# Second products of two feed-forwards as 7 quarter products in place of 8

## The chip, the cores and the metric

One Trainium2 chip, one core. The metric is the device time of one execution in microseconds (us), lower is better. Engines are written as in the profile: PE (TensorE, the products), DVE (VectorE), ACT (ScalarE), POOL (GpSimd), SP (SyncE, which issues most loads).

## The reference, cut to what matters

Two transformer blocks over 256 tokens of width 2048, everything in float32. Each ends in a feed-forward. Of the first block:

```python
z = rmsnorm(h, norm2_w) @ mlp_w1                 # (256, 2048) @ (2048, 8192)
h = h + jnp.square(jax.nn.relu(z)) @ mlp_w2      # (256, 8192) @ (8192, 2048)
```

and of the second, with 5632 hidden features and layer norms around it:

```python
g, u = jnp.split(x @ w_in, 2, axis=-1)           # (256, 2048) @ (2048, 11264)
return (jax.nn.silu(g) * u) @ w_out              # (256, 5632) @ (5632, 2048)
```

In front of these stand the mixers (gated linear attention and pooling in the first block; two kinds of attention, then attention over a memory, in the second).

## The kernel before, in words

Every product of a weight with an activation is done in three float32r products, high x high, high x low and low x high, because a float32 number is kept as a high and a low float32r part that add up to it. `Stream` (L34) loads the weights, tile by tile in the order of use, through SP's queue; a tile holds 128 partitions x 1024 numbers (512 KB). Three raw tiles are loaded ahead (`RAW`), and tiles are split up to three ahead of the product that uses them (`LOOK`, four buffers of each part): ACT copies the high part (L63), DVE subtracts it from the raw tile for the low part (L64).

The kernel first builds a list of jobs (`prog`) and then runs it. A `TJob` has the weights stationary and gives [feature, token]; it is used for a feed-forward's first product. Its tile is 2 blocks of 128 input features x 512 output features, and for each block and 128 features it issues a product of 512 columns and one of 256 (L253 to L257). An `NJob` has the activations stationary and gives [token, feature]; it is used for the second product. Its tile is 2 blocks of hidden features x 512 output features, and for both token tiles and both blocks it issues three products of 512 columns (L273 to L275), 12 a tile. Products accumulate in one of six PSUM banks (`acc`); two more banks (`aux`) belong to side work.

The hidden features of the first feed-forward are done in 8 chunks of 8 blocks of 128, those of the second in five chunks of 8 blocks and one of 4. The order is: first product of chunk c+1 (`up`, `ffn_up`), then second product of chunk c (`down`, `ffn_down`), whose rows are added to the residual `res` chunk by chunk. Four column groups of 512 make up the output's 2048 columns. Between products, `side.pump()` issues pieces of side work: results are read out of a bank in steps (`join` L346 and L360, the square or the gate, `split_steps` L371 and L373). All engines work through their instructions in the order of issue. The final layer norm's rows are loaded from POOL's queue in `last_rows` (a memset of 1.76 us on DVE at L1477).

Of the kernel before, what the change touches and what calls it, by code (L numbers as in the profile page):

```python
# [18 lines left out]
SEQ = 256  # L19
# [10 lines left out]
LOOK = 3  # L30


class Stream:
    """Weight tiles in the order in which the products use them: loaded ahead, and split  # L34
    into two float32r parts (hi + lo == w exactly)."""

    def __init__(self, nc, pool, src, specs, beside):
        self.nc, self.pool, self.src, self.specs, self.beside = nc, pool, src, specs, beside
        self.at = 0
        self.i = self.d = self.s = 0  # L40
        self.raw, self.parts = {}, {}

    def fill(self, ahead=LOOK):
        n = len(self.specs)
        nc = self.nc
        while True:
            moved = False
            if self.d < min(n, self.s + RAW):
                kq, cols, _ = self.specs[self.d]
                t = self.pool.tile([128, kq, cols], F32, name="wraw", tag="wraw", bufs=RAW)  # L50
                nc.sync.dma_start(t, bass.AP(tensor=self.src.tensor, offset=self.src.offset + self.at,
                                             ap=[[kq * cols, 128], [cols, kq], [1, cols]]))
# [5 lines left out]
            if self.s < min(n, self.i + min(ahead, 1 + self.i // 5), self.d):  # L58
                kq, cols, _ = self.specs[self.s]
                t = self.raw.pop(self.s)  # L60
                hi = self.pool.tile([128, kq, cols], F32R, name="whi", tag="whi", bufs=SPLIT)
                lo = self.pool.tile([128, kq, cols], F32R, name="wlo", tag="wlo", bufs=SPLIT)
                nc.scalar.copy(hi, t)  # L63
                nc.vector.tensor_tensor(lo, t, hi.bitcast(F32), op=OP.subtract)  # L64
                self.parts[self.s] = (hi, lo)
                self.s += 1
                moved = True
            if not moved:
                return

    def next(self, fill=True):
        self.i += 1
        if fill or self.i > self.s:
            self.fill()
        return self.parts.pop(self.i - 1)
# [10 lines left out]
class Side:  # L86
    """Work that is issued in small pieces between the products of the main sequence.
    Lanes 0 and 1 have a PSUM bank each; lane 2 is for work that needs none."""
# [11 lines left out]
    def post(self, gen):  # L100
        """A chain of steps on one result; one step at a time, chains in order."""
# [40 lines left out]
def wtile(name, kbs, pieces):  # L142
    """One weight tile: rows of the blocks kbs (consecutive), columns of pieces."""
# [9 lines left out]
def hybrid_two_block_kernel(ctx: ExitStack, tc: tile.TileContext, a, out):  # L153
# [40 lines left out]
    def early(d):  # L194
        """Loads between those of the first weights."""
# [66 lines left out]
    class NJob:  # L262
        """out[token, feature]: activations stationary, weights moving."""
# [13 lines left out]
        def run(self):  # L277
# [23 lines left out]
            # the last steps, of one group: the first token tile as a whole before the second  # L301
# [16 lines left out]
    class Call:  # L318
        """fn at this place of the sequence; what is pending is issued first."""
# [22 lines left out]

    def lo_half(b, scale=None):
# [7 lines left out]
    def join(dst, b, scale=None, rb=None):  # L351
        """dst = scale * (both halves of the bank) * rb, in two steps"""
# [16 lines left out]
    def split_steps(hi, lo, src):  # L369
        yield  # L370
        S.copy(hi, src)  # L371
        yield
        V.tensor_tensor(lo, src, hi.bitcast(F32), op=OP.subtract)  # L373

# [12 lines left out]
    def square_scale(st, eps, name):  # L387
        """Per token 1 / (mean square + eps), along the partitions."""
        def f(lane):
# [8 lines left out]
            rowb[name, "r"] = rs  # L398
        return f
# [23 lines left out]
    def turn_raw(XT, i, g):  # L423
        """Rows of the residual times a weight per feature to XT[feature, block, hi/lo, token]."""
# [16 lines left out]
    class Turn:  # L441
        """LayerNorm of the residual, in place without ln_g and ln_b, and with both to XT."""
# [49 lines left out]
        def spread(self):  # L492
            """As side work."""
# [17 lines left out]
        def begin(self):  # L511
            """At once: the first token tile while the products for the second still run."""
# [20 lines left out]
        def upto(self, n):  # L533
            """At once, as far as block pair n."""
# [8 lines left out]
    # ======================= first block =======================  # L543
# [63 lines left out]
    # pool branch  # L607
# [56 lines left out]
    # gated linear attention  # L664
# [192 lines left out]
    # output projection of the mixer  # L857
# [10 lines left out]
    def add_rows(name, turn=None, rows=None):  # L868
        """Adds to the residual, with its moments; turn: (name, weights) of what reads it next."""
# [33 lines left out]
    # feed-forward of the first block  # L903
# [21 lines left out]
    def relu2(c, at):  # L925
        def f(i, b):
            z = yield from join(None, b)
            V.scalar_tensor_tensor(z, z, 0.0, z, op0=OP.max, op1=OP.mult)
            yield from split_steps(hid[c][:, at + i, 0], hid[c][:, at + i, 1], z)
        return f  # L930

    def up(c):
        Name(set_hid, c, FCH)
        for g in range(FCH // 4):
            t_job("mlp_w1", ALLK, 128 * FCH * c + 512 * g, xt("x2t"), relu2(c, 4 * g),
# [721 lines left out]
```

## Time and profile before

| what | value |
|---|---|
| median of 3 runs | 2546.48 us (2545.93 to 2546.59) |
| span of the profiled execution, first to last instruction | 2543.4 us (its time as a run isn't recorded) |
| PE, PE weight loads, DVE, ACT, POOL busy | 2520.1, 2160.9, 1611.4, 1190.8, 60.6 us |
| weights moved | 460.77 MB of 472.93 MB, through SP's queue |
| mean granted clock of PE | 0.997 |

A busy time is the time in which at least one instruction of the engine was under way. The products overlap each other in their pipeline, so a product's listed duration is longer than the distance between the starts of two. An instruction's idle time ahead of it is named with what ended it. L12 is line 12 of the kernel.

### The profile page before, as it was taken

To read this page: it belongs to the slowest core of one execution; us is meant where nothing else is said; L and a number is where in the kernel's file an instruction comes from. 1 tells how busy PE (TensorE), PEld (TensorE's weight loads), DVE (VectorE), ACT (ScalarE), POOL (GpSimd) and SP (SyncE) were. 2 spreads that over 40 slices of the span, in tenths; PEclk is the share of its full clock that TensorE was granted. 3 is DMA by queue.
4 is the path that set the end of the run, shared out by engine and by line. 5 is a ranking of instruction groups with operands and counts; after the bars stand their busy time and mean duration, and the time that the engine had idled before them with its cause. 6 is when DMAs were issued, how large, how long until landed. Compare 5 with 4: busy or idle time off the path is not lost.

```text
span 2543.4 us, 34921 instructions
## 1 busy us (share of the span) xinstructions
PE 2520.1 (99%) x13581; PEld 2160.9 (85%) x13581; DVE 1611.4 (63%) x2240; ACT 1190.8 (47%) x1680; POOL 60.6 (2%) x82
## 2 busy tenths in 40 slices
PE   8999999999999999999999999999999999999998
PEld 8897888888888888888888888888788888888886
DVE  5655666556656656768656667767775555565557
ACT  5444444444444444444544565555544444444443
POOL 0000000000000000000000000020200000000000
PEclk9999999999999999999999999999999999999999
DMA  8444555555566565555555555665566666566664
GB/s 278 133 160 147 164 190 189 191 191 191 183 198 197 190 193 190 187 168 181 172 174 166 166 185 188 224 218 165 190 190 190 193 189 195 186 197 189 193 193 156
DMA packets 132326, 472.93 MB, mean 186 GB/s; under 512 B 14992, under 2 KB 16352, under 8 KB 131888
## 3 DMA queue, kind: packets, MB, share of 16 engines
q1 hardware_dynamic: 128624, 460.77, 56.5%
q0 software_dynamic: 3104, 9.32, 1.3%
q8 instruction: 106, 1.74, 0.3%
q10 hardware_dynamic: 432, 0.61, 0.1%
q14 instruction: 60, 0.49, 0.1%
HBM read 468.54 MB, written 2.10 MB: 185 GB/s over the span
## 4 chain that ended last, share of the span: by engine, by line
PE 96%; DVE 2%; DMA 1%; ACT 1%; issue 0%; POOL 0%; SPq 0%; DVEq 0%; ACTq 0%; POOLq 0%
PE acc L257 34%; PE acc L256 17%; PE acc L273 11%; PE acc L274 11%; PE acc L275 11%; PE acc L253 2%; PE acc L247 2%; PE acc L249 2%; PE acc L248 2%; DMA wraw<-in_weights_dram 1%; PE acc L254 1%; DVE wlo L64 1%; PE aux L1160 0%; PE aux L1090 0%; ACT whi L63 0%
## 5 line engine op out<-in xcount | busy, mean ns | idle before, releaser
L64 DVE TENSOR_TENSOR wlo<-wraw,whi 128x1024 fp32r<-128x1024 f32 (+1 forms) x870 | 1055.6, 1219 | 856.0 <-ACT whi L63 854.6
L63 ACT CAST whi<-wraw 128x1024 fp32r<-128x1024 f32 (+1 forms) x870 | 905.8, 1047 | 1060.4 <-PE acc L257 507.7
L257 PE MATMUL acc<-x5t,whi 128*128 128x512 f32 x1320 | 462.8, 394 | 1.0 <-DVE x5t L490 1.0
L256 PE MATMUL acc<-x5t,wlo 128*128 128x256 f32 x1320 | 366.7, 278 | 0.0
L257 PE MATMUL acc<-x3t,whi 128*128 128x512 f32 x960 | 339.4, 395 | 0.0
L257 PE MATMUL acc<-x2t,whi 128*128 128x512 f32 x960 | 335.9, 394 | 0.0
L257 PEld LDWEIGHTS acc<-x5t,whi 128*128 128x128 f32 x1320 | 247.8, 188 | 54.7 <-DVE x5t L490 1.4
L256 PE MATMUL acc<-x3t,wlo 128*128 128x256 f32 x960 | 272.0, 283 | 0.0
L256 PE MATMUL acc<-x2t,wlo 128*128 128x256 f32 x960 | 266.1, 277 | 0.0
L256 PEld LDWEIGHTS acc<-x5t,wlo 128*128 128x128 f32 x1320 | 248.1, 188 | 4.3 <-DVE wlo L64 0.2
L257 PEld LDWEIGHTS acc<-x2t,whi 128*128 128x128 f32 x960 | 180.0, 187 | 39.0
L257 PEld LDWEIGHTS acc<-x3t,whi 128*128 128x128 f32 x960 | 180.1, 188 | 38.6
L273 PE MATMUL acc<-whi,hid 128*128 128x512 f32 x512 | 199.5, 390 | 0.0
L274 PE MATMUL acc<-wlo,hid 128*128 128x512 f32 x512 | 199.2, 389 | 0.0
L275 PE MATMUL acc<-whi,hid 128*128 128x512 f32 x512 | 199.2, 389 | 0.0
L256 PEld LDWEIGHTS acc<-x3t,wlo 128*128 128x128 f32 x960 | 181.0, 189 | 3.2
L256 PEld LDWEIGHTS acc<-x2t,wlo 128*128 128x128 f32 x960 | 180.2, 188 | 2.9
L274 PE MATMUL acc<-wlo,fh 128*128 128x512 f32 x352 | 137.1, 389 | 0.5 <-DVE wlo L64 0.5
L273 PE MATMUL acc<-whi,fh 128*128 128x512 f32 x352 | 137.0, 389 | 0.0
L275 PE MATMUL acc<-whi,fh 128*128 128x512 f32 x352 | 136.9, 389 | 0.0
L275 PEld LDWEIGHTS acc<-whi,hid 128*128 128x128 f32 x512 | 96.1, 188 | 20.0
L274 PEld LDWEIGHTS acc<-wlo,hid 128*128 128x128 f32 x512 | 96.1, 188 | 19.9
(481 smaller groups left out, 3577.5 us busy)
## 6 DMA issues: line engine op xcount, KB each, us to landing
wraw<-in_weights_dram SPq DMA_DIRECT2D x859, 512.0 KB, 3.6
row<-in_ln_g_dram POOLq DMA_DIRECT2D x12, 256.0 KB, 6.5
wraw<-in_weights_dram SPq DMA_DIRECT2D x8, 336.0 KB, 2.9
ht<-in_hT_dram SPq DMA_DIRECT2D x8, 272.0 KB, 5.1
res<-in_x_dram SPq DMA_DIRECT2D x2, 1024.0 KB, 8.6
row<-in_ln_b_dram POOLq DMA_DIRECT2D x8, 256.0 KB, 9.3
out_dram<-res SPq DMA_DIRECT2D x6, 256.0 KB, 2.7
pw<-in_pool_w_dram SPq DMA_DIRECT2D x1, 1024.0 KB, 8.7
```

What stands on the lines that cost most here:

```text
L63: nc.scalar.copy(hi, t)
L64: nc.vector.tensor_tensor(lo, t, hi.bitcast(F32), op=OP.subtract)
L247: mm(b[:m, :n], wh, x[:, 0], start=first, stop=False)
L248: mm(b[:m, :n], wh, x[:, 1], start=False, stop=False)
L249: mm(b[:m, :n], wl, x[:, 0], start=False, stop=last)
L253: mm(bv, wh, x, start=True, stop=False, skip_group_check=True)
L254: mm(bv[:, 1], wl, x[:, 0], start=False, stop=False, skip_group_check=True)
L256: mm(bv[:, 1], wl, x[:, 0], start=False, stop=False, skip_group_check=True)
L257: mm(bv, wh, x, start=False, stop=last, skip_group_check=True)
L273: mm(b, xh, hi[:, j, :n], start=first, stop=False)
L274: mm(b, xh, lo[:, j, :n], start=False, stop=False)
L275: mm(b, xl, hi[:, j, :n], start=False, stop=last)
```

## The change

In 15 places, two column groups of a chunk's second product (256 tokens x 1024 hidden features x 1024 output columns) are done as a 2x2 matrix of quarters: four quarters of the activations (128 tokens x 512 hidden features) and four of the weights (512 x 512), with 7 products of quarters (`seven`). Three of these products use sums of weight quarters and four use sums of activation quarters. In the first feed-forward it is column groups 0 and 1 of chunks 0 to 6 (7 places; groups 2 and 3 go on as before in `row_units`), in the second all columns of chunks 0 to 3 (8 places). The last chunks stay as they were.

- The four weight quarters stay in SBUF (`Ring`: five slots of 1 MB, a sixth and later quarter is loaded where an earlier one is done with), are summed in place by DVE, and each product's quarter is split into high and low as the tiles were (`Item`, `Stream.fill`). The sums that a tile needs are issued one tile early, between the high and the low part of the tile in front.
- The sums of activation quarters are made as the hidden features arrive (`four_sums`) and split later (`convert`).
- Products that share a bank leave one product or more between the read of the bank (`put`) and the next product into it. What is common to three output quarters is kept in `u` over all chunks and added once (`add_common`, `add_common_scaled`).
- A first product is done one block of 128 output features at a time (`feature_units`: tiles of 8 input blocks x 128), and its tiles are placed between the steps of `seven` (`merge`).
- The row factor 2^0.25 of the second block's residual goes into the affine step, `last_rows` is issued after the last chunk's first product, and its loads follow each other at a pause of 1 where it was 6.

```diff
 class Stream:
...
+            if self.q < len(self.quads) and self.s > self.quads[self.q].after:
+                q = self.quads[self.q]
+                q.t = q.slot()
+                self.load(q.t, q.at, *q.spec[:2])
+                self.q += 1
                 moved = True
+            if self.s < min(n, self.i + min(ahead, 1 + self.i // 5)):
...
+                    hi = self.pool.tile([128, kq, cols], F32R, name="whi", tag="whi", bufs=SPLIT)
+                    lo = self.pool.tile([128, kq, cols], F32R, name="wlo", tag="wlo", bufs=SPLIT)
+                    nc.scalar.copy(hi, t)
+                    self.pre(self.s + 1)
+                    nc.vector.tensor_tensor(lo, t, hi.bitcast(F32), op=OP.subtract)
+                    if held:
+                        self.sums(it.post)
...
+    def feature_units(W, c0, rhs, evac):
...
+                for j in range(8):
+                    x = rhs(8 * h + j)
+                    wh, wl = hi[:, j], lo[:, j]
...
+                        mm(bv[:, 1], wl, x[:, 0], start=False, stop=False, skip_group_check=True)
+                        mm(bv, wh, x, start=False, stop=h == 1 and j == 7, skip_group_check=True)
...
+    def seven(W, k0, c0, ring, lhs, put):
+        b12, b11, b22, b21 = ring.quads(W, k0, c0)
+        add, sub = OP.add, OP.subtract
+        at = {}
+
+        def unit(name, h, bank, first, then):
+            def run():
+                hi, lo = stream.next()
+                if first and h == 0:
+                    at[bank] = aux(0) if bank == "y" else aux(1) if bank == "x" else acc()
+                b = at[bank]
+                for j in range(2):
+                    xh, xl = lhs(name, 2 * h + j)
+                    mm(b, xh, hi[:, j], start=first and h == 0 and j == 0, stop=False, skip_group_check=True)
+                    mm(b, xh, lo[:, j], start=False, stop=False, skip_group_check=True)
+                    mm(b, xl, hi[:, j], start=False, stop=h == 1 and j == 1, skip_group_check=True)
+                    if h == 1 and j == 1:
+                        put(then, b)
+                    side.pump()
+            return run
+
+        out = []
+        for name, bank, first, then, item in (
+                ("s1", "y", True, "-22", lambda h: Item(b12[h], pre=[(b12[h], b11[h], add)])),
+                ("a11", "x", True, "u", lambda h: Item(b11[h])),
+                ("s2", "u", True, "u+", lambda h: Item(b12[h], pre=[(b12[h], b22[h], add)])),
+                ("a12", "x", False, "+11", lambda h: Item(b21[h], post=[(b21[h], b12[h], add)])),
+                ("s3", "w", True, "-22", lambda h: Item(b12[h], pre=[(b12[h], b11[h], sub)])),
+                ("s4", "y", False, "-12", lambda h: Item(b22[h])),
+                ("a22", "w", False, "+21", lambda h: Item(b21[h]))):
+            for h in range(2):
+                out.append(Unit(item(h), unit(name, h, bank, first, then)))
+        return out
+
+    def merge(head, first, second, tail):
+        n = len(second) - tail
+        done = 0
+        for k, u in enumerate(second):
+            upto = len(first) if k >= n else min(len(first), head + (len(first) - head) * k // max(n - 1, 1))
+            prog.extend(first[done:upto])
...
+    def four_sums(where, i, u, l):
...
+        V.tensor_tensor(sf[:, 0, i], l1, u1, op=OP.subtract)
+        V.scalar_tensor_tensor(sf[:, 1, i], sf[:, 0, i], -1.0, u0, op0=OP.mult, op1=OP.subtract)
+        V.scalar_tensor_tensor(sf[:, 2, i], l0, -1.0, sf[:, 1, i], op0=OP.mult, op1=OP.subtract)
+        V.tensor_tensor(sf[:, 3, i], u0, u1, op=OP.subtract)
...
+    def middle(c):
+        Name(set_hid, c + 1, FCH)
+        ups = up_parts(c + 1)
+        down = seven("mlp_w2", FCH * c, 0, mring, lambda name, j: quarter(sums, hid[c], name, j), put_scaled(c))
+        merge(3 if c == 0 else 2, ups[:SHARE], down, 0)
+        rows = [u for g in (2, 3) for u in row_units("mlp_w2", FCH * c, g, lambda kb: hid[c][:, kb], add_scaled)]
+        merge(1, ups[SHARE:], rows, 2)
...
+    def ffn_middle(c):
+        Name(set_fh, c + 1, chunks[c + 1][1])
+        down = [x for p in range(2) for x in
+                seven("w_ffn_out_2", 8 * c, 1024 * p, ring, lambda name, j: quarter(fh, fh[c], name, j), put_rows(c, p))]
+        merge(5 if c == 0 else 3, up_units(c + 1), down, 4)
...
+    ffn_up()
+    last = len(chunks) - 1
+    Name(lambda: side.finish(tk["affine"]))
+    for c in range(last - 1):
+        ffn_middle(c)
+    Name(set_fh, last, 1)
+    prog.extend(up_units(last))
+    Call(add_common)
+    Name(last_rows)
+    n_job("w_ffn_out_2", range(8 * last - 8, 8 * last), grp, lambda kb: fh[last - 1][:, kb - 8 * last + 8], add_part)
+    n_job("w_ffn_out_2", range(8 * last, 8 * last + 4), grp, lambda kb: fh[last][:, kb - 8 * last], final_rows, tail=2)
```

## Rows read from the trace of the kernel before

**Rows 1.** The page's parts 1 and 2: busy time by engine, PE's clock.

```profile
PE 2520.1 (99%) x13581; PEld 2160.9 (85%) x13581; DVE 1611.4 (63%) x2240; ACT 1190.8 (47%) x1680; POOL 60.6 (2%) x82
...
PEclk9999999999999999999999999999999999999999
```

**Rows 2.** The page's part 4: the chain that ended last, by engine.

```profile
PE 96%; DVE 2%; DMA 1%; ACT 1%; issue 0%; POOL 0%; SPq 0%; DVEq 0%; ACTq 0%; POOLq 0%
```

**Rows 3.** Busy time by stretch: both feed-forwards with several chunks each.

```profile
core 0: us, PE busy (x) PEld busy (x) DVE busy (x) ACT busy (x) POOL busy (x), PEclk, DMA share, GB/s
...
425.00:1043.00 618.00, 618.00 (x3103) 524.36 (x3102) 381.57 (x462) 270.98 (x340) 0.00 (x0) 1.00 0.59 190
...
1978.00:2460.00 482.00, 482.00 (x2545) 413.35 (x2544) 274.06 (x320) 217.32 (x285) 0.00 (x0) 1.00 0.61 191
```

**Rows 4.** Timeline of PE in a second product: first and last of 36 products.

```profile
620.00 0.39 PE L273 MATMUL acc<-whi,hid 128*128 128x512 f32 x1
...
627.93 0.39 PE L275 MATMUL acc<-whi,hid 128*128 128x512 f32 x1
```

**Rows 5.** Timeline of ACT in a first product: first and last of five copies.

```profile
560.90 1.05 ACT L63 CAST whi<-wraw 128x1024 fp32r<-128x1024 f32 x1 [1.73 <-PE acc L257]
...
571.99 1.05 ACT L63 CAST whi<-wraw 128x1024 fp32r<-128x1024 f32 x1 [1.72 <-PE acc L257]
```

**Rows 6.** Timeline of PE and ACT where a second product begins.

```profile
426.24 0.40 PE L257 MATMUL acc<-x2t,whi 128*128 128x512 f32 x1
...
426.47 0.39 PE L273 MATMUL acc<-whi,hid 128*128 128x512 f32 x1
...
434.88 1.05 ACT L63 CAST whi<-wraw 128x1024 fp32r<-128x1024 f32 x1 [0.69 <-PE acc L275]
```

**Rows 7.** Groups of DVE's instructions by form: busy us, mean ns of one.

```profile
L64 DVE TENSOR_TENSOR wlo<-wraw,whi 128x1024 fp32r<-128x1024 f32 x859 | 1047.0, 1224 | 849.6 <-ACT whi L63 848.2
L360 DVE TENSOR_TENSOR ev<-acc,ev 128x256 f32<-128x256 f32 x124 | 51.7, 417 | 0.0
L944 DVE SCALAR_TENSOR_TENSOR res<-acc,rq,res 128x512 f32<-128x512 f32 x56 | 39.3, 743 | 0.0
...
L940 DVE TENSOR_TENSOR res<-acc,res 128x512 f32<-128x512 f32 x32 | 20.6, 682 | 0.0
...
L1114 DVE SCALAR_TENSOR_TENSOR pb<-l1c,pb 128x128 f32<-128x128 f32 x1 | 0.3, 291 | 0.0
...
L1113 DVE TENSOR_TENSOR l1c<-l1c,pb 128x128 f32<-128x128 f32 x1 | 0.3, 282 | 0.0
```

**Rows 8.** Timeline of DVE, 430 to 438 us: instructions without idle time between.

```profile
430.97 0.42 DVE L360 TENSOR_TENSOR ev<-acc,ev 128x256 f32<-128x256 f32 x1
431.42 0.42 DVE L928 SCALAR_TENSOR_TENSOR ev<-ev 128x256 f32<-128x256 f32 x1
431.76 0.98 DVE L373 TENSOR_TENSOR hid<-ev,hid 128x256 fp32r<-128x256 f32 x2
433.27 2.36 DVE L64 TENSOR_TENSOR wlo<-wraw,whi 128x1024 fp32r<-128x1024 f32 x2 [0.53 <-ACT whi L63]
...
437.11 1.40 DVE L944 SCALAR_TENSOR_TENSOR res<-acc,rq,res 128x512 f32<-128x512 f32 x2
```

**Rows 9.** Groups of ACT's instructions by form: the high parts.

```profile
L63 ACT CAST whi<-wraw 128x1024 fp32r<-128x1024 f32 x859 | 898.3, 1051 | 1048.7 <-PE acc L257 507.7 <-PE acc L275 328.0 <-DMA wraw<-in_weights_dram 134.9
```

**Rows 10.** Loads (KB each, median us to landing), and one stretch's busy times.

```profile
wraw<-in_weights_dram SPq DMA_DIRECT2D x859, 512.0 KB, 3.6
row<-in_ln_g_dram POOLq DMA_DIRECT2D x12, 256.0 KB, 6.5
...
2475.00:2500.00 25.00, 24.48 (x108) 19.96 (x107) 14.83 (x15) 10.97 (x10) 0.00 (x0) 1.00 0.67 233
```

**Rows 11.** Timeline of DVE at the last layer norm's preparation.

```profile
2466.00 1.76 DVE L1477 MEMSET gb<- 64x2048 f32 x1 [0.37 <-issue]
```

More of the change, by code (lines that the diff above doesn't have):

```diff
@@ new lines, in add_common_scaled, with row_units, unit, run @@
+    def add_common_scaled():
+        u = sums["u"][0]
+        for t, g, k in ((1, 0, "r"), (0, 1, "-r"), (1, 1, "-r")):
+            r = res[:, t, 512 * g:512 * g + 512]
+            V.scalar_tensor_tensor(r, u, rowb["x2t", k][t], r, op0=OP.mult, op1=OP.add)
+    def row_units(W, k0, g, lhs, evac):
+        bs = {}
+        def unit(i):
+            def run():
+                hi, lo = stream.next()
+                for t in range(2):
+                    if i == 0:
+                        bs[t] = acc()
+                    for j in range(2):
+                        x = lhs(2 * i + j)
+                        xh, xl = x[:, 0, t * 128:t * 128 + 128], x[:, 1, t * 128:t * 128 + 128]
+                        mm(bs[t], xh, hi[:, j], start=i == j == 0, stop=False)
+                        mm(bs[t], xh, lo[:, j], start=False, stop=False)
+                        mm(bs[t], xl, hi[:, j], start=False, stop=i == 3 and j == 1)
+                    if i == 3:
+                        evac(g, t, bs[t])
+                    side.pump()
+                    side.pump()
+            return run
+        return [Unit(wtile(W, range(k0 + 2 * i, k0 + 2 * i + 2), [grp[g]]), unit(i)) for i in range(4)]
@@ new lines, in put_gate, with f, put_up @@
+    def put_gate(i):
+        def f(b):
+            d = fh["sg", i] = tmp(i % 2, "c", [128, SEQ])
+            yield from join(d, b)
+            for _ in range(4):
+                yield
+            S.activation(d, d, AF.Silu)
+        return f
+    def put_up(c, i, pair, last):
+        def f(b):
+            z = yield from join(None, b)
+            V.tensor_tensor(z, z, fh["sg", i], op=OP.mult)
+            if pair and i < 4:
+                fh["z"] = z
+            elif pair:
+                four_sums(fh, i - 4, fh["z"], z)
+                if last:
+                    side.post(convert(fh, (0, 1)))
+            yield from split_steps(fh[c][:, i, 0], fh[c][:, i, 1], z, 3)
+        return f
@@ new lines, in up_units, with put_rows, f @@
+    def up_units(c):
+        g0, n = chunks[c]
+        order = [i + 4 * k for i in range(4) for k in range(n)]
+        out = []
+        for i in order:
+            c0 = 512 * g0 + 128 * i
+            out += feature_units("w_ffn_in_2", c0, xt("x5t"), put_gate(i))
+            out += feature_units("w_ffn_in_2", FF + c0, xt("x5t"), put_up(c, i, c < len(chunks) - 2, i == order[-1]))
+        return out
+    ring = Ring(new_slots(lambda: side.finish(tk["affine"])))
+    def put_rows(c, p):
+        def f(what, b):
+            u = fh["u"][p]
+            if what == "-22" and fh["last"] != c:
+                fh["last"] = c
+                side.post(convert(fh, (3, 2)))
+            if what == "u" and c == 0:
+                V.tensor_copy(u, b)
+            elif what[0] == "u":
+                V.tensor_tensor(u, b, u, op=OP.add)
+            else:
+                r = res[:, int(what[1]) - 1, 1024 * p + 512 * (int(what[2]) - 1):][:, :512]
+                if what[0] == "+":
+                    V.tensor_tensor(r, b, r, op=OP.add)
+                else:
+                    V.scalar_tensor_tensor(r, b, -1.0, r, op0=OP.mult, op1=OP.add)
+        return f
@@ L1572, in hybrid_two_block_kernel @@
     Call(finish)
[L1574 to L1575 removed]
+    stream = Stream(nc, wp, a["weights"], [s for j in prog for s in j.specs], early, LEAD)
     for j in prog:
         j.run()
[L1578 removed]
+    return stream.specs
 _SHAPES = {
```

309 lines of the change are left out of this document (242 added, 67 removed).

## The prediction

> **What bounds the kernel now.** I read the page first, then the chain of waits, the busy time by stretch, the timelines of single tiles, and the groups by form. TensorE (PE) is busy in 99% of the span, and the chain that ends last runs through PE for 96% [rows 1, 2]. The stretches of both feed-forwards show PE busy for 618.00 of 618.00 us and 482.00 of 482.00 us at a granted clock of 1.00 (the upper level, 2.4 GHz), with VectorE (DVE) at 62% and 57% and ScalarE (ACT) at 44% and 45% [rows 3]. So the change pays if it takes work from PE, until DVE has as much as PE.
>
> "Busy" isn't the price of a product. A 128x512 product is listed with 0.39 us, but products start closer: 35 starts from 620.00 to 627.93 us, so 0.2266 us each [rows 4]. A tile of a second product has 12 of them, 2.72 us. A tile of a first product shows in the spacing of the high parts that ACT makes from it: four from 560.90 to 571.99 us, 2.77 us each [rows 5].
>
> **What is removed.** One pair is two column groups of 512 in one chunk of 8 feature blocks: 2 groups x 8 blocks x 2 token tiles x 3 = 96 products. The new form has 7 x 4 blocks x 3 = 84. So 12 x 0.2266 = 2.72 us of PE go per pair, 40.8 us for the 15 pairs: 7 in the first feed-forward (one a chunk; column groups 2 and 3 stay in eight old tiles), 8 in the gated one (two a chunk). Without new waits this is the whole gain.
>
> **What is added, on DVE above all.** A pair had 8 tiles to split into high and low parts; it now has 14 half-size steps (two per product, 6 x 0.2266 = 1.36 us of PE each), and every one splits a full 128x1024 tile: 6 more copies on ACT, 6 more subtractions on DVE. Then 8 in-place sums of weight quarters on DVE. ACT has room: 6 x 1.05 = 6.3 us a pair [rows 9] in stretches where it idles over half.
>
> DVE prices, from start to start, since that is what a queue pays: two low parts run in 2.36 us with 1.22 for the last, so 1.14; a scaled add of 512 columns out of PSUM 0.67 (1.40 less 0.74); an operation of 256 columns 0.34, or 0.45 where the next one needs its result [rows 7, 8]. A plain add of 512 out of PSUM is then 0.68 - 0.07 = 0.61. The four sums of activations per feature block are 128x128 operations of 0.28 to 0.29 us, three of them in a chain: about 1.2 us [rows 7]. No row shows the sum of two weight quarters. The low part is the nearest (same 1024 elements, two SBUF sources): 1.14. From below, 0.86 ns an element as in the memset of 2048, 0.88 us [rows 11]; from above 1.25, its full 1.22 and a wait.
>
> The Trainium skill, VectorE: DVE Perf Modes (the DRAIN you can't avoid), says that the next operation does not start until the pipeline is empty, though it allows an earlier start where nothing holds it. By the strict form a low part costs 1.22 and the change ends at 2568 (third rival); by the row it costs 1.14 and the sum is 2528. The row of two low parts in 2.36 us speaks for the early start.
>
> **First feed-forward, one pass (7 of them).** 12 first-product tiles lie between the 14 half steps, four lie between the eight old tiles.
> - Merged part, PE: 12 x 2.77 + 14 x 1.36 = 52.3 us. DVE: 26 low parts 29.6, 8 sums 9.1, six feature blocks' results at 1.24 (0.45 + 0.45 + 0.34) 7.4, seven reads of banks 4.6, two blocks' four sums 2.4, a late conversion 0.6: 53.7 us. So DVE is the fuller one here.
> - Eight old tiles and four first-product ones: PE 32.8 us, DVE some 24. PE sets the pace and DVE gets ahead again.
> How far ahead? The stream splits three tiles ahead. The high part of tile n+4 begins 0.25 us after PE leaves tile n: the first second-product tile begins at 426.47, three tiles of 2.72 later PE leaves the third, at 434.63, and the copy that waited for it starts at 434.88 [rows 4, 6]. High part 1.05, low part 1.14, about 0.1 for the signals: 2.6 us. Three merged tiles last 5.9 us on average. So DVE can fall behind by 3.3 us before PE waits.
> How far behind? A product with sums (s1, s2, a12, s3) has 6.98 us of PE (2 half steps and 1.54 first-product tiles) and 8.23 of DVE: +1.25. One without (a11, s4, a22) 5.95: -1.03. In their order (s1, a11, s2, a12, s3, s4, a22) the debt is 3.97 after s3. By then four of the six blocks' results and both groups of four sums have fallen due, 1.1 more than the even share, and 0.6 of conversions: 5.7. Less 3.3, PE waits 2.4 us a pass around s3; I take 2.5. The saving of 2.72 shrinks to 0.2 a pass, 1.5 us for 7. With a sum at 0.88 the debt falls by 6 x 0.26 and the wait to 0.9 (gain 13); with 1.25 it is 3.2 (loss 3).
>
> **Gated feed-forward, one pass (4 of them).** PE: 32 first-product tiles and 28 half steps, 88.6 + 38.1 = 126.7 us where it had 88.6 + 43.5; 5.43 saved. DVE: 60 low parts 68.4, 16 sums 18.2, eight blocks' gate and up results 12.7, 14 reads 8.5, four blocks' four sums 4.8, conversions 2.5: 115 us. PE stays ahead on average, and in the run s2, a12, s3 it is 28.2 of DVE to 29.1 of PE, inside the slack. The weak place is the end of a pass, where the last half steps run without first-product tiles between: the last block's result and four sums (0.9 + 1.2) come in one piece there, then a read of 0.6, and then the low part of the last step: it ends at about 9.4 us, counted from the start of the last first-product tile, and PE wants it at 2.77 + 4 x 1.36 = 8.2. A wait of 1.2 us in three of the four passes (the last prepares no sums): 3.6.
> After the gated pairs the common part is added to three quarters in each half of the columns, six adds of 0.6, in front of the 1.76 us memset [rows 11], with the last block's chain forced out first: about 0.9 us late against three tiles' 8.2. In the first feed-forward three such adds have the cover of old tiles: nothing.
> Sum: 4 x 5.43 - 3.6 - 0.9 = 17.2 us.
>
> **At nothing.** First-product tiles of 8 blocks x 128 columns have the same products in the same bytes; PE shows no gap where the two kinds of product meet (426.24, 426.47) [rows 6]. The output rows' factor 2^0.25 moves into the affine step, operation for operation. The bytes loaded are the same, each quarter once. A read of a bank has another product (2.7 us or more) before that bank is written again; without that, PE would wait 0.6 to 0.7 plus a latency per read. The last norm's rows now come from POOL's queue in one burst of 1 MB (a pause of 1 for 6) in the stretch that shows 233 GB/s at 67% of the DMA engines [rows 10]; three raw tiles cover it, or 2 us if they don't. Quarter loads go through SP's queue with the others: 7 of 512 KB can come due together when s4 frees its slot, 3.7 MB; at that rate 16 us, with the three loaded and three split tiles ahead of them as cover.
>
> **Sum.** 1.5 + 17.2 = 18.7 us off the profiled span of 2543.4: 2524.7. Runs are 3.1 us above the span (2546.48), so 2528.
>
> **Rivals.**
> 1. DVE never makes PE wait. For it: the page's mean of 63% for DVE, a lead that I took from average tiles, the low price of a sum. Against it: 53.7 to 52.3 us in the merged part. Then 2546.5 - 40.8 = 2506.
> 2. Loads come late: SP's queue is one, a quarter that waits for its slot holds the raw tiles behind it. For it: landings of 6.5 us where other loads run beside, against 3.6 [rows 10]; against it, the same bytes in 97 to 98% of the time. With 1.2 us per pair, 15 x 1.2 = 18 goes: 2546, no change.
> 3. Slower: each DVE operation takes its whole listed duration, because most of the new ones wait for another engine's signal. That is 0.08 us more for each of some 47 operations up to s3, 3.8 us, so PE waits 6.3 a pass and the first feed-forward loses 7 x 3.6 = 25; the gated one keeps some 1 us a pass, 4: 2546.5 + 21 = 2568. It decides from a wait of 5.2 us a pass on, where 7 x (S - 2.72) eats 17.2. Against it stand the starts 1.14 apart.
> 4. The change doesn't save what it counts: reads of the banks, in order behind DVE's late work, hold the next product of the same bank. 0.8 us in each of 15 pairs leaves 2540.
>
> **How the numbers follow.** Forecast 0.50 (2518 to 2541 its own range, from the two prices of a sum and the end-of-pass waits); rival 1 0.17; rival 2 0.13; rival 3 0.12; rival 4 0.08. Below 2541.4 (0.2%, about what a measurement can tell) lie 0.47 of the forecast, all of rival 1 and half of rival 4: 0.68. Within 0.2%: 0.03, 0.10 of rival 2, 0.04 of rival 4, 0.01 of rival 3: 0.18. Slower: 0.11 and 0.03: 0.14. The range takes in rival 1 and rival 2 and leaves out rival 3: 2505 to 2553.
>
> **What would show it.** PE: 180 second products fewer, 2.72 us less per pair, and in the first feed-forward waits of PE for low parts (DVE) of about 2.5 us a pass around s3, none in the eight old tiles. DVE over 95% busy in the merged parts there, about 90% in the gated one, with PE's waits only at the ends of passes. No wait of PE for a bank, and few of DVE for quarter loads. Wrong would be: no PE waits at all (rival 1); ACT or DVE waiting for loads (2); waits over 5 us a pass with DVE starts 1.22 apart (3).

## The result and the profile after

The changed kernel takes 2574.51 us (median of 4 runs, 2572.19 to 2578.55) where the kernel before took 2546.2 beside it: ratio 1.0112, 95% interval 1.0098 to 1.0126. It is 28 us slower; 2528 was forecast, with 2505 to 2553 as the range. The profiled execution took 2575.55 us, its span is 2573.8.

First the page of the changed kernel, parts 1 and 4 (busy time by engine; the chain by engine), against [rows 1, 2]:

```profile
PE 2512.9 (98%) x13401; PEld 2135.6 (83%) x13401; DVE 1941.0 (75%) x2745; ACT 1304.2 (51%) x1825; POOL 58.3 (2%) x82
...
PE 77%; DVE 13%; DMA 5%; ACT 2%; issue 2%; SPq 0%; POOL 0%; DVEq 0%; ACTq 0%; POOLq 0%
```

The 180 products are gone (13581 to 13401), and the chain now runs for 13% through DVE and for 5% through loads. Next the busy time by stretch, columns as in [rows 3]:

```profile
394.00:404.00 10.00, 6.75 (x16) 4.98 (x17) 8.33 (x16) 6.93 (x12) 0.00 (x0) 0.50 0.28 97
...
425.00:1043.00 618.00, 602.18 (x2985) 499.60 (x2986) 512.31 (x677) 314.82 (x400) 2.19 (x4) 1.00 0.54 186
...
484.00:540.00 56.00, 54.36 (x279) 45.04 (x278) 55.24 (x72) 31.62 (x41) 0.00 (x0) 1.00 0.43 148
540.00:575.00 35.00, 34.01 (x165) 28.11 (x164) 22.66 (x34) 16.18 (x21) 0.00 (x0) 1.00 0.73 255
...
1978.00:2460.00 482.00, 478.33 (x2523) 406.75 (x2522) 417.64 (x508) 275.87 (x356) 0.00 (x0) 1.00 0.57 193
```

PE was busy for all of both feed-forwards' stretches. Now it isn't: 15.8 us are missing in the first, 3.7 in the gated one. In a merged part (484 to 540) DVE is busy for 55.24 of 56.00 us; behind it (540 to 575) it has time, and the DMA engines are at 73%. From 394 to 404 TensorE got half its clock.

The place of the loss is read best from stretches cut at PE's own products. "First" below runs from the first product with x2t to the last with hid, "gated" from the first with x5t to the last with fh, us of the profiled execution; the last column is the median time and its ratio to the kernel before, measured beside it (2545.8 to 2546.8).

| kernel | first | gated | time, ratio [95%] |
|---|---|---|---|
| before | 706.7 | 733.8 | 2546.2 |
| changed | 732.2 | 737.5 | 2574.5, 1.0112 [1.0098, 1.0126] |
| forecast for it | 705.2 | 716.6 | 2528 |
| tiles_alone | 712.1 | 739.7 | 2558.2, 1.0045 [1.0032, 1.0057] |
| no_weight_sums | 707.9 | 737.3 | 2549.5, 1.0013 [1.0004, 1.0022] |
| loads_spread | 717.8 | 737.7 | 2561.3, 1.0058 [1.0045, 1.0070] |
| turns | 733.1 | 735.6 | 2571.2, 1.0099 [1.0085, 1.0112] |
| share16 | 710.1 | 737.7 | 2552.5, 1.0027 [1.0018, 1.0036] |
| two_banks | 741.6 | 732.9 | 2579.4, 1.0130 [1.0117, 1.0144] |
| share_and_loads | 703.2 | 739.4 | 2547.3, 1.0001 [0.9992, 1.0010] |
| all_four | 703.6 | 724.5 | 2531.9, 0.9942 [0.9928, 0.9955] |
| gated_alone | 706.7 | 722.4 | 2535.9, 0.9957 [0.9945, 0.9970] |
| one_bank_first | 699.6 | 726.0 | 2529.3, 0.9931 [0.9919, 0.9944] |
| head_six | 702.9 | 724.5 | 2533.8, 0.9946 [0.9933, 0.9958] |

So the first feed-forward lost 25.5 us where 1.5 were to be gained, the gated one 3.7 where 17.2 were; the rest of the span differs by 1.2.

Four places in the trace say how. **The turn into the first pass**: timelines of DVE, ACT and PE.

```profile
382.87 0.42 DVE L541 TENSOR_TENSOR ev<-acc,ev 128x256 f32<-128x256 f32 x1
...
395.53 0.28 DVE L522 TENSOR_TENSOR sf<-l1c 128x128 f32<-128x128 f32 x1
...
394.99 0.62 ACT L1130 CAST spa<-sf 128x512 fp32r<-128x512 f32 x1 [2.44 <-DVE sf L519]
...
395.66 0.79 PE L482 MATMUL aux<-whi,spa 128*128 128x512 f32 x1 [4.96 <-ACT spa L1130]
...
398.47 0.80 PE L484 MATMUL aux<-whi,spa 128*128 128x512 f32 x1 [1.59 <-DVE spa L1135]
```

The last old tile of the first chunk hands over four blocks' results at once. Their joins, rebuilt values and four sums fill DVE's queue from 382.87 to 395.81, with one sum and one low part of weights between. The first product with a converted sum waits for them. Behind the stop the granted clock is 0.50, and products that were listed with 0.39 us are listed with 0.63.

**Behind a merged part**: timelines of SP's queue, ACT, DVE and PE.

```profile
529.38 0.43 SPq L80 DMA_DIRECT2D quads<-in_weights_dram  x1
529.86 0.43 SPq L80 DMA_DIRECT2D quadf<-in_weights_dram  x1
532.27 0.33 SPq L80 DMA_DIRECT2D wraw<-in_weights_dram  x1
532.94 0.33 SPq L80 DMA_DIRECT2D quads<-in_weights_dram  x1
533.32 0.97 SPq L80 DMA_DIRECT2D quadf<-in_weights_dram  x2
534.33 0.99 SPq L80 DMA_DIRECT2D quade<-in_weights_dram  x2
...
545.00 1.05 ACT L127 CAST whi<-wraw 128x1024 fp32r<-128x1024 f32 x1 [4.17 <-DMA wraw<-in_weights_dram]
...
546.08 1.23 DVE L129 TENSOR_TENSOR wlo<-wraw,whi 128x1024 fp32r<-128x1024 f32 x1 [5.97 <-ACT whi L127]
...
551.13 0.39 PE L434 MATMUL acc<-x2t,wlo 128*128 128x256 f32 x1 [0.99 <-DVE wlo L129]
```

Seven quarter loads go out between 529.38 and 535.32, as soon as s4 lets go of its two half slots, with one raw tile between. The next raw tiles land late, ACT waits 4.17 us for one, DVE is idle for 5.97, right after a part in which its timeline marks no idle time.

**An end of a pass in the gated feed-forward**: DVE and PE.

```profile
2048.55 0.29 DVE L519 TENSOR_TENSOR sf<-ev 128x128 f32<-128x128 f32 x1
...
2049.62 0.68 DVE L1848 SCALAR_TENSOR_TENSOR res<-acc,res 128x512 f32<-128x512 f32 x1
...
2050.45 0.47 PE L482 MATMUL acc<-whi,fh 128*128 128x512 f32 x1 [1.21 <-DVE res L1848]
```

The read of s3's bank stands behind the last block's four sums, and a22, which adds to the same bank, waits for it.

**The last norm's rows**: ACT and PE.

```profile
2502.45 1.90 ACT L1886 CAST ro<-gb 64x2048 fp32r<-64x2048 f32 x1 [10.22 <-DMA gb<-in_ln_b_dram]
...
2498.02 0.50 PE L342 MATMUL acc<-wlo,fh 128*128 128x512 f32 x1 [1.26 <-DVE wlo L129]
2505.35 0.49 PE L341 MATMUL acc<-whi,fh 128*128 128x512 f32 x1 [1.78 <-ACT whi L127]
2506.61 0.79 PE L342 MATMUL acc<-wlo,fh 128*128 128x512 f32 x1 [0.77 <-DVE wlo L129]
```

With a pause of 1 the copy of the rows comes so early in ACT's queue that it waits 10.22 us for their loads, and the high parts of weights wait behind it. The first of the three waits of PE, at 2498.02, has another cause: the low part stands in DVE's queue behind the six adds of the common part and the memset.

### The profile page after: what moved, and what is told of

Read it like the earlier page. It is cut to its first block, busy times and chain, and to the rows that moved or that the text cites. A ratio compares the mean times of both kernels' runs of the same rounds, so it can differ in the third digit from the quotient of the medians.

```text
span 2573.8 us, 35138 instructions
## 1 busy us (share of the span) xinstructions
PE 2512.9 (98%) x13401; PEld 2135.6 (83%) x13401; DVE 1941.0 (75%) x2745; ACT 1304.2 (51%) x1825; POOL 58.3 (2%) x82
## 4 chain that ended last, share of the span: by engine, by line
PE 77%; DVE 13%; DMA 5%; ACT 2%; issue 2%; SPq 0%; POOL 0%; DVEq 0%; ACTq 0%; POOLq 0%
PE acc L325 15%; PE acc L435 13%; PE acc L324 8%; PE acc L434 6%; DVE wlo L129 6%; DMA wraw<-in_weights_dram 5%; PE acc L342 5%; PE acc L341 5%; PE acc L343 5%; ACT whi L127 2%; PE acc L315 1%; PE acc L317 1%; PE acc L316 1%; PE aux L484 1%; PE aux L482 1%
## 5 line engine op out<-in xcount | busy, mean ns | idle before, releaser
L129 DVE TENSOR_TENSOR wlo<-wraw,whi 128x1024 fp32r<-128x1024 f32 (+2 forms) x750 | 908.2, 1216 | 523.5 <-ACT whi L127 513.1
L127 ACT CAST whi<-wraw 128x1024 fp32r<-128x1024 f32 (+2 forms) x750 | 780.0, 1045 | 653.7 <-PE acc L325 226.2
L435 PE MATMUL acc<-x5t,whi 128*128 128x512 f32 x1080 | 387.6, 399 | 0.0
L434 PEld LDWEIGHTS acc<-x2t,wlo 128*128 128x128 f32 x840 | 159.0, 189 | 25.5 <-DVE wlo L129 22.3
L527 ACT COPY ev<-acc 128x256 f32<-128x256 f32 x256 | 94.0, 371 | 162.8 <-PE acc L435 143.7
L129 DVE TENSOR_TENSOR wlo<-quads,whi 128x1024 fp32r<-128x1024 f32 x86 | 104.9, 1220 | 13.4 <-ACT whi L127 5.4
L127 ACT CAST whi<-quads 128x1024 fp32r<-128x1024 f32 x86 | 90.2, 1051 | 44.8 <-DVE quads L85 40.8
L315 PE MATMUL acc<-x1t,whi 128*128 128x272 f32 (+1 forms) x336 | 100.5, 299 | 6.3 <-ACT whi L127 5.5
L129 DVE TENSOR_TENSOR wlo<-quadf,whi 128x1024 fp32r<-128x1024 f32 x78 | 95.1, 1219 | 12.0 <-ACT whi L127 7.0
L127 ACT CAST whi<-quadf 128x1024 fp32r<-128x1024 f32 x78 | 82.0, 1051 | 33.3 <-DVE quadf L85 28.3
L317 PE MATMUL acc<-x1t,wlo 128*128 128x272 f32 (+1 forms) x336 | 98.1, 292 | 0.0
L316 PE MATMUL acc<-x1t,whi 128*128 128x272 f32 (+1 forms) x336 | 97.8, 291 | 0.0
```

The costliest lines, as they stand in the source:

```text
L315: mm(b[:m, :n], wh, x[:, 0], start=first, stop=False)
L316: mm(b[:m, :n], wh, x[:, 1], start=False, stop=False)
L317: mm(b[:m, :n], wl, x[:, 0], start=False, stop=last)
L434: mm(bv[:, 1], wl, x[:, 0], start=False, stop=False, skip_group_check=True)
L435: mm(bv, wh, x, start=False, stop=h == 1 and j == 7, skip_group_check=True)
```

## The experiments

Each is the changed kernel with one edit, unless it says otherwise. Stretches and times are in the table above.

**tile_forms.** The kernel before; the first products of its first feed-forward in several forms, one for each chunk.

```diff
+    FORMS = {1: {}, 2: {"banks": 2}, 3: {"moving": 2}, 4: {"strided": True},
+             5: {"banks": 2, "moving": 2, "strided": True}, 6: "wide"}
```

> The kernel before, with the first products of the first feed-forward's chunks written in other forms, one form a chunk; chunks 0 and 7 stay as they are. Chunk 1: tiles of 8 feature blocks by 128 columns, as in the changed kernel. Chunk 2: the same, but the products go to two PSUM banks by turns of two pairs. Chunk 3: the same as chunk 1, but only two different activation blocks are read in a tile, by turns (wrong products). Chunk 4: as chunk 1, but the weight blocks of a tile are taken in the order 0, 4, 1, 5, 2, 6, 3, 7, so 2 KB apart as in the old tile (wrong products). Chunk 5: all three. Chunk 6: the old tile, but reading eight different activation blocks (wrong products). In the trace of the changed kernel a pair of first products takes 0.3524 to 0.3545 us, in that of before 0.3466, which makes 2.82 to 2.84 against 2.77 us a tile. Theory: the form of the tile costs this by itself, also without quarter products and with DVE at 62%: chunk 1 shows 2.83 a tile, chunks 0 and 7 show 2.77, and chunk 5 shows 2.77. If the single PSUM bank is what costs, chunk 2 is at 2.77 and chunks 3 and 4 at 2.83; if the eight different activation blocks cost, chunk 3 is at 2.77 and chunk 6 at 2.83; if the weights' addresses cost, chunk 4 is at 2.77. Rival: the slower pace comes from what runs beside in the changed kernel (DVE, quarter loads), and all chunks show 2.77. Whole time: some 5 tiles-of-16 sets at 16 x 0.06 = 1 us each, so 3 to 5 us over before by the theory, nothing by the rival.

One run, 2549.55 us (2546.43 beside it). PE's timeline at the edges of the 16 tiles of chunks 1, 2 and 3:

```profile
380.52 0.39 PE L365 MATMUL acc<-x2t,whi 128*128 128x512 f32 x1
...
425.70 0.39 PE L274 MATMUL acc<-whi,hid 128*128 128x512 f32 x1
...
469.22 0.39 PE L365 MATMUL acc<-x2t,whi 128*128 128x512 f32 x1
...
513.64 0.39 PE L274 MATMUL acc<-whi,hid 128*128 128x512 f32 x1
...
557.17 0.39 PE L365 MATMUL acc<-x2t,whi 128*128 128x512 f32 x1
...
602.34 0.39 PE L274 MATMUL acc<-whi,hid 128*128 128x512 f32 x1
```

45.18 us in one bank, 44.42 with two banks by turns, 45.17 with two activation blocks in place of eight. In the same way chunk 4 (other weight addresses) took 45.17, chunk 5 (all three) 44.43, chunk 6 (old tile, eight blocks) 44.39, chunk 7 (old tile) 44.40. So of the three differences the bank is the one that costs: 0.047 us a tile, when all products of a tile follow each other into one bank.

**tiles_alone.** The kernel before with that tile in 256 places and nothing else of the change.

> The kernel before with one part of the change alone: the first products of both feed-forwards, but for the first chunk of each, in tiles of 8 feature blocks by 128 columns (7 x 16 tiles in the first feed-forward, 5 chunks with 32, 32, 32, 32 and 16 in the gated one). Second products, loads and sums as before. Theory of several losses: the form of the tile costs 0.06 us a tile by itself, so (112 + 144) x 0.06 = 15 us: 2561, ratio 1.006. Rival, that the loss is all in DVE and its waits: the tiles cost nothing, 2546, ratio 1.000.

5.4 us more in the first stretch, 5.9 in the gated one; 11.8 in the medians, or 0.046 a tile. The rival falls: this part costs without any new wait.

**no_weight_sums.** A pair's 8 operations are four sums in two halves each: s1, s2, s3 and a22 use them, so four products do, and not three as the description of the change says.

```diff
-        for to, frm, op in which:
-            self.nc.vector.tensor_tensor(to.t, to.t, frm.t, op=op)
+        pass
```

> The changed kernel without the 8 sums of weight quarters of each pair on DVE (the products then take the plain quarters, so the output is wrong); products, tiles, copies, low parts, loads and slots stay. DVE loses 120 operations of 1.14 us, 9.1 us in each merged part of the first feed-forward: 44.6 against 52.3 us of PE there. Theory of several losses: only the waits of PE for DVE's low parts in the merged parts go, about 2.3 us in each of 7 passes, and the 1.4 us at three ends of passes in the gated feed-forward, together 16 to 20 us: 2555 to 2559, still slower than before; waits after the bursts of quarter loads, the slow turn into the first pass and the pace of the first products stay. Rival, that DVE's fullness is behind all of the loss: all waits go, and the 40.8 us that the 180 products saved come out: below 2520.

The first stretch falls by 24.3 us, more than the 16 expected from the merged waits, for most of the waits behind the bursts go with them: from 490 us to the stretch's end PE's only waits of over 0.2 us are three, of 0.64, 0.63 and 0.26. The gated stretch doesn't move (737.3), its ends of passes wait 1.21 as before. Still slower than before: DVE's fullness is not all of it.

**loads_spread.**

```diff
+        self.quads.sort(key=lambda q: (q.gap == 0, q.after if q.gap else 0))
...
-            if self.q < len(self.quads) and self.s > self.quads[self.q].after:
...
+            if q and self.s > q.after and (need or self.s >= self.lq + q.gap):
...
+    mring = Ring(new_slots(), 2)
```

> The changed kernel with the first feed-forward's quarter loads in the order in which their slots come free and at most one for every second weight tile, in place of a burst of seven or eight behind the last use of one slot. Same bytes, same slots, same work on every engine. Theory of several losses: the burst makes raw weight tiles late (the wait of ACT for one is 4.2 us at 545.0 in the changed kernel's trace, DVE idles 6.0 us there), which costs PE 1.3 to 1.7 us in each of 7 passes: 8 to 12 us back, 2563 to 2567. Rival, that the bursts are hidden and PE's waits there are DVE's debt from the merged part: no change, 2574.

14.4 us off the first stretch, a little more than the theory's 8 to 12, since the waits inside the merged parts shrink too. A late start of PE is the distance of two starts less the median distance. In the merged parts of passes two to six they add up to 1.8, 1.4, 1.4, 1.4 and 1.4 us, in the changed kernel to 2.3 (0.91, 0.63, 0.56 and 0.18 from 509 to 529 us), 1.4, 2.3, 2.3 and 2.7: 3.7 us of the 14.4. Behind the merged parts PE doesn't wait any more. The timeline of SP's queue shows the loads by turns now:

```profile
524.88 0.33 SPq L82 DMA_DIRECT2D wraw<-in_weights_dram  x1
525.25 0.43 SPq L82 DMA_DIRECT2D quadf<-in_weights_dram  x1
528.15 0.33 SPq L82 DMA_DIRECT2D wraw<-in_weights_dram  x1
528.53 0.42 SPq L82 DMA_DIRECT2D quade<-in_weights_dram  x1
```

**share16.**

```diff
-    SHARE = 12
+    SHARE = 16
```

> The changed kernel with all 16 first-product tiles of a pass in the first feed-forward merged between the 14 half steps (12 before), none between the eight old tiles. By my own sums the merged part then has 63.6 us of PE (14 half steps of 1.36, 16 tiles of 2.83... 64.3) to some 62 of DVE, so the debt that makes PE wait 2.3 us a pass around s3 falls by more than half. Theory that this debt is what costs in the merged parts: 7 x 1.2 to 1.5, 8 to 10 us less: 2564 to 2566. Rival, that what costs is the loads behind the merged part: with four tiles fewer there to cover them the waits for raw tiles grow, and the time is the same or longer: 2574 to 2582.

22.1 us off, over twice what I expected, and against the rival: with less cover for the loads nearly all waits behind them vanish as well. Only behind the first merged part the rival is right: there PE's late starts grow from 4.1 to 6.3 us (470 to 485 us), and one of 0.5 us stands at 727. The busy times of a merged part and of the old tiles behind it:

```profile
484.00:547.00 63.00, 63.00 (x331) 53.53 (x330) 54.20 (x73) 33.97 (x43) 0.00 (x0) 1.00 0.52 191
547.00:571.00 24.00, 24.00 (x112) 19.98 (x111) 22.14 (x31) 13.43 (x17) 0.00 (x0) 1.00 0.63 201
```

DVE has 54.20 of 63.00 us and PE never waits here. I read this so: a DVE that enters the old tiles without debt has the three tiles' lead that a burst needs.

**share_and_loads.** Both edits.

> The changed kernel with share16 and loads_spread together and nothing else. Alone, share16 took 22.1 us off the first feed-forward's stretch (732.2 to 710.1) and loads_spread 14.4 (to 717.8). Theory that both cure one loss, DVE's missing lead, which the burst of loads then turns into waits: together they take little more than share16 alone, 22 to 25 us off the stretch, the whole at 2549 to 2553. Rival, two losses side by side: 36 us off the stretch, 2538.

29.0 us off the first stretch: between the two theories' numbers. Alone the edits took 22.1 and 14.4, 36.5 together, so 7.5 us were one loss that either cures, and the rest stood side by side. Of the 29.0, 2.6 are waits of the turn itself (late starts of 9.9 us from 388 to 406 us before the edits, 7.3 with them).

**turns.** Written for both feed-forwards; the first one's lines:

```diff
             if g:
                 Call(new_sums, sums, "a")
+                for i in range(4):
+                    prog.extend(feature_units("mlp_w1", 512 * g + 128 * i, xt("x2t"),
+                                              lambda b, i=i, f=relu2(0, 4 * g, True): f(i, b)))
+                continue
```

> The changed kernel with the last first-product tiles of each feed-forward's first chunk written one block after the other (tiles of 8 blocks by 128 columns) in place of four blocks at once, so that the results, the rebuilt sums and the four sums of activations come one block at a time ahead of the first pass with seven products. Theory of several losses: in the changed kernel's trace PE waits 4.96 and 1.59 us for the converted sums at 395.7 and 398.5 and then runs 10.2 us at the lower clock, 9.9 us in all, and a like cluster of 3.6 us stands at 1933 to 1937 in the gated feed-forward; both come from four blocks' results in one piece in DVE's queue, so most of it goes: 8 to 13 us less, some 1 us back for the slower tiles: 2563 to 2568. Rival: DVE has that much work there in any order, and the wait only moves to the next tiles: 2572 to 2576.

A miss: 3.3 us in the medians. The gated cluster at 1933 is gone; the first one isn't cured. PE waits 1.60 and 2.08 us at the same two products (4.96 and 1.59 in the changed kernel), then as before for low parts (1.09 and 1.82 at 409 and 421; 0.89 and 1.83). Late starts up to 430 us fall only from 13.2 to 11.0, and the stretch is 0.9 longer. The rival's mechanism (as much work for DVE in any order) is what the first feed-forward shows.

**two_banks.** Tiles of 4 blocks by 2 x 128 columns (feature blocks i and 4 + i, or gate and up i); in the first feed-forward:

```diff
+                for q in range(4):
+                    f = q % 2
+                    bv = at["b"][f].rearrange("p (a n) -> p a n", a=2)
+                    for j in (q // 2 * 2, q // 2 * 2 + 1):
...
-            out += feature_units("mlp_w1", 128 * FCH * c + 128 * i, xt("x2t"), lambda b, f=f: f(0, b))
...
+            out += two_features("mlp_w1", c0, c0 + 512, xt("x2t"),
+                                [lambda b, f=relu2(c, i): f(0, b), later(2, lambda b, f=relu2(c, i + 4): f(0, b))])
```

> The changed kernel with the first products of two feature blocks together, in tiles of 4 blocks by 2 x 128 columns: the products go to two PSUM banks by turns of two pairs, and both results come after four tiles instead of one after every two (same products, bytes and results; DVE gets two blocks' results in one piece). Run tile_forms showed 44.42 us for 16 tiles with two banks against 45.17 with one, so 0.047 us a tile, and tiles_alone showed 11.8 us for 256 tiles in one bank. Theory: the single bank is what the form of the tile costs, so 256 x 0.047 = 12 us go, less what the larger pieces on DVE cost (two blocks' results and four sums at once, 3.7 us in place of two times 1.9, some 0.5 us a pass): 2562 to 2566. Rival: in the merged parts DVE sets the pace anyway, so the slower tiles cost nothing there, and only the gated feed-forward gets its share back, 144 x 0.047 = 7 us: 2567 to 2570.

Outside both: slower by 9.4 us in the first feed-forward. There PE now waits for a bank whose result DVE has not yet read:

```profile
635.28 0.47 PE L1279 MATMUL acc<-whi,hid 128*128 128x512 f32 x1 [2.32 <-DVE ev L575]
```

1.88 to 2.32 us in each of five passes, for the results come in pairs to a DVE that is behind. And the banks bring little where tiles alternate with half steps: in the gated passes a lone tile takes 2.81 us (median) against 2.82 with one bank, and three tiles in a row 8.32 against 8.46. In the gated feed-forward the later reading of the last block also ends the 1.21 us waits at the ends of passes; 4.6 us go there.

**all_four.** loads_spread, turns, share16, two_banks, and in the last norm's rows:

```diff
                 row_part(fh["gr"], g, c)
-                yield 1
+                yield 6
```

> The changed kernel with loads_spread, turns, share16 and two_banks together, and the last norm's rows loaded at the old pace (a pause of 6). Theory of several losses that add up: 13 us from the loads (measured), 8 to 13 from the turns, up to 10 from the merged DVE debt, 12 from the banks, 5 from the last norm's rows: 2574.5 less 45 to 50, 2525 to 2530, faster than the kernel before (ratio 0.992 to 0.994), near the time that was forecast for the change. Rival, that the losses share one cause, DVE's missing lead, so that one cure does most of the others' work: about 2574.5 less 25, 2550, not faster than before.

2531.9: the losses are several, and their cures add up, less the overlap. The time is 2 us above the theory's range. The gated stretch is 9.3 us shorter than before, where the prediction had 17.2. With the pause of 6, ACT's copy of the last norm's rows no longer waits, and of PE's three waits there only the one behind the adds is left (1.85 us at 2458.65).

**gated_alone.** The first feed-forward of the kernel before, the gated one of all_four.

> The first feed-forward as in the kernel before (old tiles, eight products); the gated feed-forward as in all_four (seven products, turn block by block, two banks, last norm's rows at the old pace). Theory that the stretches add up: 706.7 us for the first feed-forward and 724.5 for the gated one, 2535 in all, so the first feed-forward's seven products bring only 3 us even with its losses cured. Rival, that the gated stretch owes part of its 9.3 us to what stands ahead of it, or that the first one was worth more: 2540 or more.

2535.9, as the stretches said: the gated feed-forward alone brings 11.0 us.

**one_bank_first.** all_four with feature_units back in the first feed-forward.

> all_four, but the first feed-forward's first products go back to one block at a time in one PSUM bank. In two_banks the merged tiles took 2.81 us against 2.82 (median), so the two banks bring little there, while the first feed-forward's stretch grew by 9.4 us through the larger pieces on DVE. Theory that the pieces cost and the banks bring nothing there: the waits of 0.7 us in five passes and 1.4 in the first go, some 1 us comes back for the tiles: 2528 to 2530. Rival, the banks are worth their 0.047 us a tile there too, 112 x 0.047 = 5 us, and with all 16 tiles merged the pieces no longer cost: 2535 to 2537.

2529.3, the fastest of all, 17 us under before; the first stretch is 7.1 us shorter than before. The pieces cost, the banks bring nothing there. **head_six**, the other attempt on all_four:

```diff
-        merge(3 if c == 0 else 2, ups[:SHARE], down, 0)
+        merge(6 if c == 0 else 2, ups[:SHARE], down, 0)
```

> all_four, but six first-product tiles (three before) stand ahead of the first seven-product half step of the first feed-forward. In the trace of all_four PE still waits 2.5 us there for the low part of the first converted sum and then runs 3.4 us at the lower clock, and 1.4 us at 426 us. Theory: three more tiles, 8.4 us of PE, give DVE the time: the first wait and the lower clock go, 4 us: 2527 to 2529. Rival: with three tiles fewer between the half steps of that pass the debt of DVE grows by as much and the wait moves to s3: 2531 to 2533.

No difference (its interval overlaps that of all_four). The 2.5 us wait is gone. Waits of 0.73, 0.79 and 1.48 us stand at 401, 420 and 479 instead, beside one of 1.13 at 426 that was there before (1.20): the rival, a debt that moves.

## Why the prediction was wrong, step by step

- **What is removed** was right: 180 products at 0.2266 us; a second product's half step beside a first-product tile has 1.39 us (median) for the 1.36 of the forecast, 0.03 x 92 = 2.8 us for the 92 of these in the gated passes.
- **DVE's prices** were right. Weight sums are listed with 1.22 us and low parts start 1.13 apart (531.03 and 532.16, DVE's timeline below). The strict rule of the Trainium skill (VectorE: DVE Perf Modes, the DRAIN you can't avoid) would have made it 1.22; the trace keeps to the earlier start that the page allows.

```profile
531.03 1.22 DVE L129 TENSOR_TENSOR wlo<-wraw,whi 128x1024 fp32r<-128x1024 f32 x1
532.16 1.22 DVE L129 TENSOR_TENSOR wlo<-quads,whi 128x1024 fp32r<-128x1024 f32 x1
```

- **The merged part's wait** was right in place, and in size for most passes: late starts of 2.3 us in the pass shown (509 to 529 us), 1.4 to 2.7 in passes two to six and 0.2 in the last, for 2.5 forecast; DVE busy 55.24 of 56.00.

```profile
509.18 0.39 PE L434 MATMUL acc<-x2t,wlo 128*128 128x256 f32 x1 [0.75 <-DVE wlo L129]
518.32 0.39 PE L434 MATMUL acc<-x2t,wlo 128*128 128x256 f32 x1 [0.47 <-DVE wlo L129]
524.79 0.39 PE L432 MATMUL acc<-x2t,wlo 128*128 128x256 f32 x1 [0.39 <-DVE wlo L129]
```

- **The step that failed first** is the cover in "at nothing": "three loaded and three split tiles ahead" of the burst of quarter loads. I had spent that lead already, as the 3.3 us by which DVE may fall behind. Behind a merged part nothing of it is left, so the burst becomes waits (without the debt, in share16, those behind the first part stay and 0.5 us at 727, the others go; with the loads spread, all go). Debt and burst together took 29.0 us (share_and_loads) where 17.5 stood for the debt alone.
- **The second** is "PE shows no gap" for the new first-product tile. No gap, but a slower pace: 5.4 and 5.9 us (tiles_alone), since all its products go to one bank (tile_forms). That cause is shown for tiles in a row; for a tile between half steps it stays open (two_banks: 2.81 us for 2.82).
- **The third** was left out: the turn into the first pass with seven products. I priced the passes from each other and not the first from what stands ahead of it. With the two above, 706.7 - 19.0 + 5.4 = 693.1, and share_and_loads has 703.2: 10.1 us are left, and its trace shows 8 of them as late starts of PE, most between 390 and 400 us with the lower clock. The gated turn cost 3.6.
- **The fourth**: the last norm's burst, "nothing, or 2 us". The rows' loads weren't what PE felt; the copy that waits for them holds ACT's queue. Late starts of PE add up to 6.1 us there, 0.7 before. 4.6 of them come from the copy; 1.4, at 2498.02, are the wait behind the adds and the memset for which the forecast had 0.9.
- **The gated ends of passes**: 1.21 us in three passes, 4.1 with the restart, for 3.6 forecast; held by the read of a bank (rival 4's mechanism) and not by the low part. The work in DVE's queue was named rightly; that the number came out was in part luck.

The sum of the first stretch is -19.0 + 5.4 + 29.0 + 10.1 = +25.5; it closes by construction, for 10.1 is what was left. Counted in the trace alone, the late starts of at least 0.1 us add up to 38 us in the changed kernel's first stretch, to none before: -19.0 + 5.4 + 38 = +24. Gated: -21.7 + 5.9 + 4.1 + 3.6 + 5.4 + 2.8 = +0.1 of +3.7. Most of the other 3.6 are waits at the stretch's start (2.52 and 1.03 us at 1835.85 and 1843.52, for DVE's rows). They aren't owed to the change of the gated feed-forward: tile_forms, which leaves that as before, waits 2.55 and 0.98 us at the same two places and has a gated stretch 3.0 us longer than before; gated_alone, which changes it, has no wait over 0.6 us there. What brings them stays open. Of the rivals, 1 and 3 are false in their mechanism, though 3 came near in time, by luck; 2 was true of the first feed-forward, and bound to the debt; 4 was true at three places.

## What to carry to other kernels

A lead is one account: if a slower engine's debt and a burst of loads are each covered by "three tiles ahead", add them before you call either hidden, and move work between stretches until the fuller engine leaves each part without debt (one constant, 12 to 16, was worth 22 us). Price the first pass from what stands ahead of it, and ask of each copy that waits for a load what its queue holds behind it. A cure on one engine can be a loss on another: two banks made the same tiles faster alone, and the whole slower.

## What the runs showed of the hardware

- First products that follow each other into one PSUM bank take 45.17 us for 16 tiles, 44.42 when two banks take turns after every two pairs. The Trainium skill (Perfetto Trace Analysis, Optimizing Tensor Performance) advises to rotate banks so that reading overlaps the next products; here the pace alone changes, where nobody waits for a read.
- That isn't all of it: a tile with two banks that stands between half steps still takes 2.81 us in the gated passes of two_banks. What keeps it slow, the tile's order of products or its neighbours, stays open.
- After a stop of 4.96 us PE ran at a granted clock of 0.50, the lower level of 1.2 GHz, for 394 to 404 us; with a stop of 1.87 us there (one_bank_first) the same stretch has 1.00.
